# Gate and up projections turned token-major in seven of eleven groups, with a transpose through VectorE and ScalarE

## The chip, the cores and the metric

The kernel runs on one core of one Trainium2 chip. The metric is the device time of one execution in microseconds (us); the lower, the better.

The engines are named as the profile names them: PE is TensorE's matrix multiplication, PEld its weight loads, DVE is VectorE, ACT is ScalarE, POOL is GpSimd and SP is SyncE, which issues the weight transfers here.

## The reference

One layer of a decoder trunk, 256 tokens by 2048 channels, everything in float32. `D_FF` is 5632, which is eleven groups of 512 columns.

```python
def reference(x, p, ...):
    y = _rms(h, norm_mix_g[i])
    z = y @ w_in[i]                      # 2048 x 4096
    ...                                  # four mixers of 512 channels each
    h = h + jnp.concatenate([oa, ob, oc, od], axis=-1) @ w_out[i]
    y = _rms(h, norm_ffn_g[i])
    h = h + (jax.nn.silu(y @ w_gate[i]) * (y @ w_up[i])) @ w_down[i]
    y = _rms(h, norm_ple_g[i])
    h = h + jax.nn.sigmoid(y @ w_ple_gate[i]) * (p[i] @ w_ple_proj[i])
    return _rms(h, final_norm_g)
```

The change lies in the line with `w_gate`, `w_up` and `w_down`.

## The kernel before

**Numbers in two parts.** Each float32 operand is split into a high part, rounded to the format that PE multiplies in (float32r), and a low part, the rest. A product is then three matmuls: high weight by high activation, high weight by low activation, low weight by high activation. For activations `split` (line 102) does this: ACT rounds (`act`, line 66), DVE subtracts (`tt`, line 69). For weights it is done in `load_slab`.

**Slabs and steps.** All weights are streamed once. A step is one slab of weights: four K-tiles of 128 rows by 512 columns, 1 MB. `load_slab` (222) issues the transfer on SP's queue into `raw` (three buffers), has ACT write the high part `whi` (line 266, three buffers) and DVE the low part `wlo` (line 270, three buffers). `run` (398) walks the list `steps`; a slab is loaded when the step two before it begins, and after each step's matmuls `pump` takes deferred work (`defer`, 283) out of the list `bg`, up to the step's budget: it runs a piece while the credit is above minus 2.0 (`OVERDRAFT`) and takes the piece's cost off. `flush` empties the list. That is the order in which the program is written. The framework that compiles it places the waits, and may put an instruction of an engine's queue ahead of one that is written before it.

**Channel-major.** `group` (313) with `wide_out=True` multiplies one group of 512 output channels: for each K-tile `j` and each block `m` of 128 channels, line 335 loads 128 columns of the weight as the stationary operand and streams the activations. With `whi` the moving operand is the high and low part of the activation side by side, 512 columns, into one PSUM bank per `m`; with `wlo` it is the high part alone, 256 columns, into the bank's second half. That is eight matmuls for each K-tile. The result is channels by tokens, four banks a group. Even steps but the last take the 16 products with `whi` first, odd steps and the last those with `wlo`.

**Token-major.** `token_products` (389) has the tokens as the stationary operand (128 tokens of `a`) and streams 512 columns of the weight: `whi`, `wlo`, then `whi` against the low part, for one block `t` of 128 tokens. That is six matmuls of 512 columns for each K-tile and both blocks. The result is tokens by channels. In the kernel before it is used by `group_v`, the first group of the input projection, by `p_last` and by `last_a` and `last_b`, the last group of the gate of the third line.

**The feed-forward part.** `ffn` (759) is called for passes of 3, 3, 3 and 2 groups (`FFN_CUTS`). In a pass each group does four steps of `w_gate`, evacuated by `ev_gate`, and four of `w_up`, evacuated by `ev_up`, which multiplies and splits into `acts`; then four groups of `w_down` with as many steps as the pass has groups use `acts` as the moving operand, channels on the partitions. `hs` holds the split input of the pass, the normalisation's factor by token is in `stats["ffn"]`: element 0 has it with tokens on partitions, element 1 as a row repeated on all partitions. All of `xs`, `mix`, `hs`, `acts`, `hs2` and some smaller things are tiles of the pool `asp`, 28 buffers of 2 KB a partition (line 58).

Of the kernel before, what the change touches and what calls it, by code (L numbers as in the profile page):

```python
# [9 lines left out]
F32 = mybir.dt.float32  # L10
# [22 lines left out]
BUDGET = 2.8  # L33
BUDGET_OUT = 2.8
OVERDRAFT = 2.0
WARM = 9
# [15 lines left out]
def trunk(ctx: ExitStack, tc: tile.TileContext, xT, pT, par, w_in, sgu_wT, sgu_lb, sgu_b,  # L52
# [4 lines left out]
    hp_ = ctx.enter_context(tc.tile_pool(name="resid", bufs=1))  # L57
    asp = ctx.enter_context(tc.tile_pool(name="asp", bufs=28))
    rawp = ctx.enter_context(tc.tile_pool(name="rawp", bufs=3))
# [162 lines left out]
    def load_slab(i, w, k0, nk, cols, hold=False):  # L222
# [21 lines left out]
        if hold:  # L244
            load(0, nk)
            parts = []
            for s in range(nk):
                hi = asp.tile([P, 2, T], F32R, tag="a", name="hold_hi").rearrange("p a t -> p (a t)")
                lo = asp.tile([P, 2, T], F32R, tag="a", name="hold_lo").rearrange("p a t -> p (a t)")
# [14 lines left out]
        for s in range(0, nk, some):  # L264
            e = min(s + some, nk)
            act(hi[:, s:e, :n], raw[:, s:e, :n])
            if i < KD // 4:
                for k in range(4 * i + s, 4 * i + e):
                    xs.append(split(h[k], col("g_mix", k)))
            tt(lo[:, s:e, :n], raw[:, s:e, :n], hi[:, s:e, :n].bitcast(F32), ALU.subtract)  # L270
# [136 lines left out]

    xs = []
    acc1, sums1 = wk("acc", bufs=2), duo(0)
# [109 lines left out]
    def c_out(rows):  # L519
        r = both(rows())  # L520
        for q in range(2):
            tt(cv2[q], cv2[q], r, ALU.mult)
            y, sg = duo(0), duo(0)
            for a in range(2):
                i = 2 * q + a
                act(y[:, a, :], cv2[q][:, a, :], AF.Identity, bias=col("cf_lb", i),
                    scale=col("cf_g", i))
            act(sg, y, AF.Sigmoid)
            tt(y, y, sg, ALU.mult)
            for a in range(2):  # L530
                mix[8 + 2 * q + a] = split(y[:, a, :])

# [59 lines left out]
    def sgu(p, u):  # L592
# [14 lines left out]
        for a in range(2):  # L607
            mix[2 * p + a] = split(o[:, a, :])

# [24 lines left out]
    def evac_bb(p, ps):  # L634
# [5 lines left out]
        for a in range(2):  # L640
            mix[4 + 2 * p + a] = split(o[:, a, :])

# [8 lines left out]
    def pool(p, z):  # L651
# [15 lines left out]
        def project():  # L667
# [4 lines left out]
            for a in range(2):  # L672
                m = 2 * p + a
                mix[12 + m] = split(po[:, a * T:(a + 1) * T], col("pool_s", m))
        defer(0.8, project, 1)
# [47 lines left out]

    hs = [None] * KD
    acc2 = wk("acc", bufs=2)

    def out_group(g, order):
# [6 lines left out]
        def ev_last(p, ps):  # L734
# [3 lines left out]
            for j in (4 * g + 2 * p, 4 * g + 2 * p + 1):  # L738
                hs[j] = split(h[j], col("g_ffn", j))
                square(j, acc2)  # L740
# [14 lines left out]

    hs2 = [None] * KD
    acc3 = wk("acc", bufs=2)

    def ffn(g0, ng, final):
        acts = []  # L760
        gs = {}
# [13 lines left out]
        def ev_up(m, ps):  # L775
# [4 lines left out]
            tt(o, o, gs[m], ALU.mult)  # L780
            acts.append(split(o))

        h4s = lambda i: hs[4 * i:4 * i + 4]
        for g in range(g0, g0 + ng):
            group(w_gate, [(g * GW, GW)], full, h4s, ev_gate, wide_out=True,
                  hooks={i + 1: [f] for i, f in enumerate(stats_hooks(acc2, "ffn"))}
                  if g == 0 else None)
            group(w_up, [(g * GW, GW)], full, h4s, ev_up, wide_out=True)
        for g in range(4):
            def ev(m, ps, g=g):  # L790
                j = 4 * g + m
                add_residual(j, ps)
                if final:
                    hs2[j] = split(h[j], col("g_ple", j))
                    square(j, acc3)
            group(w_down, [(g * GW, GW)], [(4 * g0 + k, 4) for k in range(0, 4 * ng, 4)],
                  lambda i: acts[4 * i:4 * i + 4], ev, wide_out=True,
                  hooks={0: [(lambda: load_p()) if g == 2 else (lambda: p_tiles(0))]}
# [7 lines left out]

    psp = []

    def p_tiles(i):
        if not psp:  # L810
            for k in range(PLE // P):
                psp.append(split(pk[0][:, k, :]))
        return psp
# [35 lines left out]
    def load_g():  # L849
        t = asp.tile([P, 2, T], F32R, tag="a", name="g_row").bitcast(F32)  # L850
        g_row.append(t.rearrange("p a t -> p (a t)"))
        nc.sync.dma_start(out=g_row[0], in_=g_last.broadcast_to([P, GW]))
# [47 lines left out]
    def gate_last(t, q, ps):  # L900

        if q == 0:
            z_last[t] = asp.tile([P, 2, T], F32R, tag="a", name="z_last").bitcast(F32)
            zg_last[t] = wide()
# [107 lines left out]
```

## Time and profile before

| | us |
|---|---|
| median of three runs | 1132.54 (1131.68 to 1132.98) |
| the profiled execution | 1132.19 |
| its span, first to last instruction | 1130.5 |
| PE busy | 1118.4 (99%) |
| DVE busy | 805.5 (71%) |
| ACT busy | 585.0 (52%) |

The span is what the trace covers; 1.7 us of the profiled execution's time lie outside it. A busy share is a share of the span. The granted clock of TensorE is a mean of 0.998 of full speed. Matmuls are pipelined, so the duration of one is longer than the distance from one start to the next; it is the distance that adds up.

### The profile page before, as it was taken

Reading aid. Unit: us, or ns where it says so; the run is one execution under the profiler, and the core shown is the slowest. Engines: PE = TensorE matmul, PEld = TensorE weight load, DVE = VectorE, ACT = ScalarE, POOL = GpSimd, SP = SyncE. Lnnn points to the kernel's source line nnn. Section 1 sums busy time; section 2 is a strip of 40 time slices with the busy share of each in tenths; the row PEclk is TensorE's granted clock in tenths of the full one; section 3 lists DMA queues with packets and bytes.
Section 4 is the critical chain, followed back from the end, with each engine's and each line's share of the span. In section 5 each row is a group of like instructions: output and inputs, shape, how many; then the busy total and the mean of one; then the engine's idle time right before and its main releaser. Section 6 shows DMA issues by size and latency. Waiting matters only on the chain.

```text
span 1130.5 us, 16060 instructions
## 1 busy us (share of the span) xinstructions
PE 1118.4 (99%) x6496; PEld 990.4 (88%) x6496; DVE 805.5 (71%) x1154; ACT 585.0 (52%) x758; POOL 2.2 (0%) x15
## 2 busy tenths in 40 slices
PE   9999999999999999999999999999999999999996
PEld 7888888889888888888888888888888888889886
DVE  7789998969866675567667555766756576786685
ACT  7677677637545453334445333544533354656562
POOL 0000000000000000000000000000000000000000
PEclk9999999999999999999999999999999999999999
DMA  9855555564565646655555565465655555547642
GB/s 311 279 194 188 171 184 169 192 206 159 197 207 170 218 159 199 204 186 185 189 189 184 186 209 193 162 219 170 203 186 187 188 184 194 179 149 233 195 142 75
DMA packets 117290, 214.55 MB, mean 190 GB/s; under 512 B 4320, under 2 KB 19552, under 8 KB 117216
## 3 DMA queue, kind: packets, MB, share of 16 engines
q1 hardware_dynamic: 114640, 212.20, 56.7%
q10 hardware_dynamic: 2576, 1.32, 0.4%
q8 instruction: 51, 0.84, 0.3%
q14 instruction: 23, 0.19, 0.0%
HBM read 211.41 MB, written 2.10 MB: 189 GB/s over the span
## 4 chain that ended last, share of the span: by engine, by line
PE 95%; DVE 2%; ACT 1%; DMA 1%; issue 1%; ACTq 0%; DVEq 0%
PE ps_mm L335 88%; PE ps_mm L338 2%; PE ps_mm L394 1%; PE ps_mm L395 1%; PE ps_mm L393 1%; PE ps_mm L340 1%; DVE wlo L70 1%; ACT whi L67 1%; DMA wide<-sgu_lb 0%; DMA h<-xT 0%; DVE cv L70 0%; ACT duo L67 0%; PE ps_po L670 0%; DVE duo L70 0%; PE ps_sum L190 0%
## 5 line engine op out<-in xcount | busy, mean ns | idle before, releaser
L335 PE MATMUL ps_mm<-a,whi 128*128 128x512 f32 x2944 | 692.0, 391 | 0.2 <-DVE duo L70 0.2
L335 PEld LDWEIGHTS ps_mm<-a,whi 128*128 128x128 f32 x2944 | 544.9, 188 | 109.3 <-DVE duo L70 0.4
L70 DVE TENSOR_TENSOR wlo<-raw,whi 128x2048 fp32r<-128x2048 f32 (+2 forms) x205 | 452.3, 2207 | 249.1 <-ACT whi L67 246.1
L67 ACT ACTIVATE whi<-raw 128x2048 fp32r<-128x2048 f32 (+2 forms) x205 | 378.6, 1847 | 321.6 <-PE ps_mm L335 222.8
L335 PEld LDWEIGHTS ps_mm<-a,wlo 128*128 128x128 f32 x2944 | 368.1, 191 | 8.5
L335 PE MATMUL ps_mm<-a,wlo 128*128 128x256 f32 x2944 | 371.9, 283 | 0.0
L67 ACT ACTIVATE short<-ps_mm 128x256 f32<-128x256 f32 x100 | 37.5, 375 | 79.4 <-PE ps_mm L335 77.9
L70 DVE TENSOR_TENSOR h<-ps_mm,h 128x256 f32<-128x256 f32 (+1 forms) x168 | 61.6, 426 | 3.4 <-PE ps_mm L335 2.9
L70 DVE TENSOR_TENSOR short<-ps_mm,short 128x256 f32<-128x256 f32 x100 | 41.9, 419 | 24.0 <-ACT short L67 22.9
L67 ACT ACTIVATE short<-short 128x256 f32<-128x256 f32 x56 | 23.2, 414 | 64.6 <-DVE short L70 64.5
L70 DVE TENSOR_TENSOR short<-short,r 128x256 f32<-128x256 f32 x100 | 42.3, 423 | 17.7 <-ACT short L67 16.0
L67 ACT ACTIVATE duo<-long_duo,prm 128x256 f32<-128x256 f32 x108 | 45.3, 498 | 1.5 <-DVE duo L70 1.1
L70 DVE TENSOR_TENSOR cv<-cv,duo 128x512 f32<-128x512 f32 x54 | 37.0, 689 | 3.7 <-ACT duo L67 0.7
L70 DVE TENSOR_TENSOR short<-short 128x256 f32<-128x256 f32 x88 | 37.3, 424 | 2.6
L67 ACT ACTIVATE a<-h,prm 128x256 fp32r<-128x256 f32 x32 | 16.0, 501 | 19.6 <-DVE h L70 19.3
L393 PE MATMUL ps_mm<-whi,a 128*128 128x512 f32 (+1 forms) x72 | 25.3, 360 | 0.7 <-ACT a L67 0.7
L394 PE MATMUL ps_mm<-wlo,a 128*128 128x512 f32 (+1 forms) x72 | 25.3, 356 | 0.1
L395 PE MATMUL ps_mm<-whi,a 128*128 128x512 f32 (+1 forms) x72 | 25.3, 356 | 0.0
L338 PE MATMUL ps_mm<-a,whi 128*128 128x256 f32 x88 | 21.5, 283 | 0.0
L340 PE MATMUL ps_mm<-a,whi 128*128 128x256 f32 x88 | 21.5, 284 | 0.0
L67 ACT ACTIVATE a<-short 128x256 fp32r<-128x256 f32 x44 | 17.0, 412 | 3.5 <-DVE short L70 3.5
L67 ACT ACTIVATE short<-h 128x256 f32<-128x256 f32 x41 | 16.5, 403 | 2.7 <-DVE h L70 2.7
(135 smaller groups left out, 397.1 us busy)
## 6 DMA issues: line engine op xcount, KB each, us to landing
raw<-w_gate SPq DMA_DIRECT2D x44, 1024.0 KB, 5.0
raw<-w_up SPq DMA_DIRECT2D x44, 1024.0 KB, 5.0
raw<-w_down SPq DMA_DIRECT2D x44, 1024.0 KB, 5.0
raw<-w_in SPq DMA_DIRECT2D x20, 1024.0 KB, 5.3
raw<-w_out SPq DMA_DIRECT2D x16, 1024.0 KB, 5.1
raw<-w_pg SPq DMA_DIRECT2D x16, 1024.0 KB, 5.1
raw<-w_in SPq DMA_DIRECT2D x36, 256.0 KB, 5.1
raw<-w_in SPq DMA_DIRECT2D x6, 512.0 KB, 6.6
```

The source lines that it names most:

```text
L67: nc.scalar.activation(out, in_, func, bias=bias, scale=scale)
L70: nc.vector.tensor_tensor(out=out, in0=a, in1=b, op=op)
L335: nc.tensor.matmul(o, w, r, start=first, stop=final)
L338: nc.tensor.matmul(o, w, a[:, 0, :], start=first, stop=final and low == 1)
L340: nc.tensor.matmul(o, w, a[:, 1, :], start=False, stop=final)
L393: nc.tensor.matmul(ps, a[:, 0, c], whi[:, x], start=start and j == 0, stop=False)
L394: nc.tensor.matmul(ps, a[:, 0, c], wlo[:, x], start=False, stop=False)
L395: nc.tensor.matmul(ps, a[:, 1, c], whi[:, x], start=False, stop=stop and j == len(tiles) - 1)
```

## The change

Of each pass all groups but the last do gate and up token-major (`group_t`): 2, 2, 2 and 1, together seven of eleven. The last group of each pass stays as it was. `ev_gate_t` and `ev_up_t` evacuate 128 tokens by 512 channels at a time and work on whole banks, with the normalisation's factor as a scalar of the partition. `ev_up_t` rounds and subtracts there, has DVE turn the high and the low part in square blocks of 32 by 32 into `turned`, and defers four pieces for each block of tokens. A piece, `move`, is four ACT copies of 32 partitions by 256 elements, which bring the blocks to the partitions where `w_down` needs them. The steps of the feed-forward groups get a budget of 2.0, and a piece is entered at a cost of 1.0. `hidden` flushes what is left before `w_down` reads. The pool `asp` is cut into 7 buffers of 8 KB instead of 28 of 2 KB, each buffer a quad of four split tiles, and every user of the pool names its place in a quad.

```diff
+BUDGET_FFN = 2.0
-    asp = ctx.enter_context(tc.tile_pool(name="asp", bufs=28))
+    asp = ctx.enter_context(tc.tile_pool(name="asp", bufs=7))
...
+    def quad():
+        return asp.tile([P, 4, 2, T], F32R, tag="a", name="a")
+    class Quads:
+        def __init__(self):
+            self.q = {}
+        def __getitem__(self, k):
+            if k // 4 not in self.q:
+                self.q[k // 4] = quad()
+            return self.q[k // 4][:, k % 4]
-    def split(src, scale=None):
-        a = asp.tile([P, 2, T], F32R, tag="a", name="a")
+    def split(src, a, scale=None):
...
+    def group_t(w, g, evac, hooks=None):
+        ps = []
+        def body(i, parts):
+            if i == 0:
+                ps.extend(bank() for _ in range(TT))
+            for t in range(TT):
+                token_products(ps[t], t, hs[4 * i:4 * i + 4], parts, i == 0, i == 3)
+                if i == 3:
+                    evac(t, ps[t])
+            for f in (hooks or {}).get(i, ()):
+                f()
+        for i in range(KD // 4):
+            steps.append(((w, 4 * i, 4, [(g * GW, GW)]), lambda p, i=i: body(i, p), BUDGET_FFN))
...
+        def ev_gate_t(t, ps):
+            r = stats["ffn"][0][:, t:t + 1]
+            s = wide()
+            act(s, ps, AF.Sigmoid, scale=r)
+            gs[t] = wide()
+            stt(gs[t], ps, r, s, ALU.mult, ALU.mult)
+        def ev_up_t(n):
+            turned = []
+            def f(t, ps):
+                if not turned:
+                    turned.append(asp.tile([P, TT, 2, GW], F32, tag="a", name="turned"))
+                o, hi = gs[t], wide()
+                stt(o, ps, stats["ffn"][0][:, t:t + 1], o, ALU.mult, ALU.mult)
+                act(hi.bitcast(F32R), o)
+                tt(o, o, hi, ALU.subtract)
+                nc.vector.transpose(out=turned[0][:, t, 0, :], in_=hi)
+                nc.vector.transpose(out=turned[0][:, t, 1, :], in_=o)
+                for i in range(4):
+                    defer(1.0, lambda i=i: move(n, t, i, turned[0]))
+            return f
+        def move(n, t, i, turned):
+            acts[4 * n]
+            c = slice(t * P + 32 * i, t * P + 32 * i + 32)
+            for j in range(4):
+                act(acts.q[n][32 * j:32 * j + 32, :, :, c].rearrange("p m s b -> p s m b"),
+                    turned[32 * i:32 * i + 32, t].rearrange(
+                        "p s (m j b) -> p s m j b", m=4, j=4)[:, :, :, j, :])
+        def hidden(i):
+            if bg:
+                flush()
+            return [acts[k] for k in range(4 * i, 4 * i + 4)]
...
-        for g in range(g0, g0 + ng):
-            group(w_gate, [(g * GW, GW)], full, h4s, ev_gate, wide_out=True,
-                  hooks={i + 1: [f] for i, f in enumerate(stats_hooks(acc2, "ffn"))}
-                  if g == 0 else None)
-            group(w_up, [(g * GW, GW)], full, h4s, ev_up, wide_out=True)
+        for n, g in enumerate(range(g0, g0 + ng)):
+            hooks = ({i + 1: [f] for i, f in enumerate(stats_hooks(acc2, "ffn"))}
+                     if g == 0 else None)
+            if n < ng - 1:
+                group_t(w_gate, g, ev_gate_t, hooks)
+                group_t(w_up, g, ev_up_t(n))
+            else:
+                group(w_gate, [(g * GW, GW)], full, h4s, ev_gate, BUDGET_FFN, wide_out=True)
+                group(w_up, [(g * GW, GW)], full, h4s, ev_up, BUDGET_FFN, wide_out=True)
```

## Rows read from the trace of the kernel before

**Rows 1.** Page, busy time: us, share of the span, instructions.

```profile
PE 1118.4 (99%) x6496; PEld 990.4 (88%) x6496; DVE 805.5 (71%) x1154; ACT 585.0 (52%) x758; POOL 2.2 (0%) x15
PEclk9999999999999999999999999999999999999999
```

**Rows 2.** Chain that ended last: by line, then one piece (start, us).

```profile
PE ps_mm L335 88%; PE ps_mm L338 2%; PE ps_mm L394 1%; PE ps_mm L395 1%; PE ps_mm L393 1%; PE ps_mm L340 1%; DVE wlo L70 1%; ACT whi L67 1%; DMA wide<-sgu_lb 0%; DMA h<-xT 0%; DVE cv L70 0%; ACT duo L67 0%; PE ps_po L670 0%; DVE duo L70 0%; PE ps_sum L190 0%
...
302.98 714.31 PE ps_mm L335 x4108
```

**Rows 3.** Timeline of PE, 495 to 550: start, us, instruction, count.

```profile
498.19 4.00 PE L335 MATMUL ps_mm<-a,wlo 128*128 128x256 f32 x32
502.02 7.47 PE L335 MATMUL ps_mm<-a,whi 128*128 128x512 f32 x32
509.33 4.00 PE L335 MATMUL ps_mm<-a,wlo 128*128 128x256 f32 x32
513.16 7.44 PE L335 MATMUL ps_mm<-a,whi 128*128 128x512 f32 x32
520.44 4.00 PE L335 MATMUL ps_mm<-a,wlo 128*128 128x256 f32 x32
...
546.50 3.82 PE L335 MATMUL ps_mm<-a,whi 128*128 128x512 f32 x16
```

**Rows 4.** Timeline of PE, `last_a`: first and after the last of 48 matmuls.

```profile
1096.98 0.39 PE L393 MATMUL ps_mm<-hold_hi,a 128*128 128x512 f32 x1
...
1107.86 0.50 PE L190 MATMUL ps_sum<-ones,acc 128*128 128x1 f32 x4
```

**Rows 5.** Timeline of PE, end of `group_v`: first and after the last of 18 matmuls.

```profile
24.78 0.39 PE L393 MATMUL ps_mm<-whi,a 128*128 128x512 f32 x1
...
28.90 0.62 PE L335 MATMUL ps_mm<-a,whi 128*128 128x512 f32 x2
```

**Rows 6.** Windows of Rows 3, 5 and 4: length, busy us by engine, clock, DMA.

```profile
502.02:546.50 44.48, 44.48 (x258) 39.34 (x257) 29.30 (x37) 20.71 (x24) 0.00 (x0) 1.00 0.56 189
24.78:28.90 4.12, 4.12 (x20) 3.38 (x18) 4.08 (x5) 2.24 (x2) 0.00 (x0) 1.00 0.67 210
1096.98:1107.86 10.88, 10.88 (x49) 9.01 (x48) 7.87 (x17) 6.75 (x14) 0.00 (x0) 1.00 0.00 0
```

**Rows 7.** Groups of ACT by form: count, busy us, mean ns, idle before.

```profile
L67 ACT ACTIVATE whi<-raw 128x2048 fp32r<-128x2048 f32 x191 | 365.6, 1914 | 321.3 <-PE ps_mm L335 222.8 <-DVE h L70 36.5 <-issue 33.1
L67 ACT ACTIVATE a<-short 128x256 fp32r<-128x256 f32 x44 | 17.0, 412 | 3.5 <-DVE short L70 3.5
L67 ACT ACTIVATE wide<-wide 128x512 f32<-128x512 f32 x6 | 3.7, 620 | 0.2 <-DVE wide L70 0.2
L67 ACT ACTIVATE wide<-ps_mm,rsy 128x512 f32<-128x512 f32 x2 | 1.3, 670 | 0.0
```

**Rows 8.** Groups of DVE by form, same columns.

```profile
L70 DVE TENSOR_TENSOR wlo<-raw,whi 128x2048 fp32r<-128x2048 f32 x191 | 437.4, 2290 | 244.3 <-ACT whi L67 241.9 <-DMA raw<-w_in 2.0
L76 DVE SCALAR_TENSOR_TENSOR wide<-wide 128x512 f32<-128x512 f32 x2 | 1.4, 687 | 0.0
L70 DVE TENSOR_TENSOR wide<-wide 128x512 f32<-128x512 f32 x2 | 1.4, 685 | 0.0
```

**Rows 9.** Timeline of ACT, 495 to 550, around the end of a gate group.

```profile
503.15 0.38 ACT L67 ACTIVATE short<-ps_mm 128x256 f32<-128x256 f32 x1 [2.85 <-PE ps_mm L335]
504.48 0.42 ACT L67 ACTIVATE short<-short 128x256 f32<-128x256 f32 x1 [0.95 <-DVE short L70]
504.81 0.36 ACT L67 ACTIVATE short<-ps_mm 128x256 f32<-128x256 f32 x1
505.92 1.91 ACT L67 ACTIVATE whi<-raw 128x2048 fp32r<-128x2048 f32 x1 [0.75 <-ACT short L67]
507.74 0.40 ACT L67 ACTIVATE short<-short 128x256 f32<-128x256 f32 x1
```

**Rows 10.** Timeline of ACT: two copies back to back; a copy and its successor.

```profile
530.37 0.71 ACT L67 ACTIVATE a<-short 128x256 fp32r<-128x256 f32 x2
...
1084.54 0.42 ACT L67 ACTIVATE short<-short 128x256 f32<-128x256 f32 x1 [2.20 <-DVE short L70]
1084.87 0.61 ACT L67 ACTIVATE hold_hi<-raw 128x512 fp32r<-128x512 f32 x1
```

More of the change, by code (lines that the diff above doesn't have):

```diff
@@ L245, in load_slab @@
             load(0, nk)
-            parts = []
+            parts, kept = [], Quads()
             for s in range(nk):
-                hi = asp.tile([P, 2, T], F32R, tag="a", name="hold_hi").rearrange("p a t -> p (a t)")
-                lo = asp.tile([P, 2, T], F32R, tag="a", name="hold_lo").rearrange("p a t -> p (a t)")
+                hi, lo = (kept[2 * s + b].rearrange("p a t -> p (a t)") for b in range(2))
                 act(hi, raw[:, s, :])
@@ L268, in load_slab @@
                 for k in range(4 * i + s, 4 * i + e):
-                    xs.append(split(h[k], col("g_mix", k)))
+                    xs.append(split(h[k], x_parts[k], col("g_mix", k)))
             tt(lo[:, s:e, :n], raw[:, s:e, :n], hi[:, s:e, :n].bitcast(F32), ALU.subtract)
@@ L406, in run @@
             pump(budget)
-    xs = []
+    xs, x_parts, mix_parts = [], Quads(), Quads()
     acc1, sums1 = wk("acc", bufs=2), duo(0)
@@ L530, in c_out @@
             for a in range(2):
-                mix[8 + 2 * q + a] = split(y[:, a, :])
+                mix[8 + 2 * q + a] = split(y[:, a, :], mix_parts[8 + 2 * q + a])
     def gelu2(z, s, g):
@@ L607, in sgu @@
         for a in range(2):
-            mix[2 * p + a] = split(o[:, a, :])
+            mix[2 * p + a] = split(o[:, a, :], mix_parts[2 * p + a])
     hb, cb = {}, {}
@@ L640, in evac_bb @@
         for a in range(2):
-            mix[4 + 2 * p + a] = split(o[:, a, :])
+            mix[4 + 2 * p + a] = split(o[:, a, :], mix_parts[4 + 2 * p + a])
     def evac_d(p, ps):
@@ L673, in project @@
                 m = 2 * p + a
-                mix[12 + m] = split(po[:, a * T:(a + 1) * T], col("pool_s", m))
+                mix[12 + m] = split(po[:, a * T:(a + 1) * T], mix_parts[12 + m], col("pool_s", m))
         defer(0.8, project, 1)
@@ L722, in add_residual @@
         tt(h[j], ps[:, T:], h[j], ALU.add)
-    hs = [None] * KD
+    hs, h_parts = [None] * KD, Quads()
     acc2 = wk("acc", bufs=2)
@@ L738, in ev_last @@
             for j in (4 * g + 2 * p, 4 * g + 2 * p + 1):
-                hs[j] = split(h[j], col("g_ffn", j))
+                hs[j] = split(h[j], h_parts[j], col("g_ffn", j))
                 square(j, acc2)
@@ L753, in trunk @@
             out_group(g, k_order)
-    hs2 = [None] * KD
+    hs2, h2_parts = [None] * KD, Quads()
     acc3 = wk("acc", bufs=2)
+    def group_t(w, g, evac, hooks=None):
[11 more added lines that the diff above has]
+            steps.append(((w, 4 * i, 4, [(g * GW, GW)]), lambda p, i=i: body(i, p), BUDGET_FFN))
     def ffn(g0, ng, final):
-        acts = []
+        acts = Quads()
         gs = {}
@@ L780, in ev_up @@
             tt(o, o, gs[m], ALU.mult)
-            acts.append(split(o))
-        h4s = lambda i: hs[4 * i:4 * i + 4]
-        for g in range(g0, g0 + ng):
-            group(w_gate, [(g * GW, GW)], full, h4s, ev_gate, wide_out=True,
-                  hooks={i + 1: [f] for i, f in enumerate(stats_hooks(acc2, "ffn"))}
-                  if g == 0 else None)
-            group(w_up, [(g * GW, GW)], full, h4s, ev_up, wide_out=True)
+            split(o, acts[4 * (ng - 1) + m])
+        def ev_gate_t(t, ps):
[4 more added lines that the diff above has]
+            stt(gs[t], ps, r, s, ALU.mult, ALU.mult)
@@ L793, in ev @@
                 if final:
-                    hs2[j] = split(h[j], col("g_ple", j))
+                    hs2[j] = split(h[j], h2_parts[j], col("g_ple", j))
                     square(j, acc3)
             group(w_down, [(g * GW, GW)], [(4 * g0 + k, 4) for k in range(0, 4 * ng, 4)],
-                  lambda i: acts[4 * i:4 * i + 4], ev, wide_out=True,
+                  hidden, ev, wide_out=True,
                   hooks={0: [(lambda: load_p()) if g == 2 else (lambda: p_tiles(0))]}
@@ L804, in trunk @@
         g0 += ng
-    psp = []
+    psp, p_parts = [], Quads()
     def p_tiles(i):
@@ L811, in p_tiles @@
             for k in range(PLE // P):
-                psp.append(split(pk[0][:, k, :]))
+                psp.append(split(pk[0][:, k, :], p_parts[k]))
         return psp
@@ L849, in load_g @@
     def load_g():
-        t = asp.tile([P, 2, T], F32R, tag="a", name="g_row").bitcast(F32)
-        g_row.append(t.rearrange("p a t -> p (a t)"))
+        g_row.extend(asp.tile([P, 4, GW], F32, tag="a", name="g_row")[:, i] for i in range(4))
         nc.sync.dma_start(out=g_row[0], in_=g_last.broadcast_to([P, GW]))
@@ L902, in gate_last @@
         if q == 0:
-            z_last[t] = asp.tile([P, 2, T], F32R, tag="a", name="z_last").bitcast(F32)
+            z_last[t] = g_row[1 + t].rearrange("p (a t) -> p a t", a=2)
             zg_last[t] = wide()
```

## The prediction

> **What bounds the kernel now.** I read the busy times first: PE has 1118.4 us of a span of 1130.5, 99%, at full granted clock in every slice; VectorE has 71%, ScalarE 52% [rows 1]. The chain that ended last confirms that PE is not merely busy but the path: 88% of the span are the channel-major matmuls of line 335, and the feed-forward part, the stretch that is changed, is one unbroken piece of 714.31 us and 4108 matmuls [rows 2]. Nothing there ever makes PE wait. So two questions decide: does PE need less time for the same products, and does the new work on the other engines make PE wait where it did not?
>
> **What a channel-major step costs.** The timeline of PE shows blocks of 32 equal matmuls, half a block belonging to one step and half to the next. From the start of the block at 502.02 to the same place one group of gate and up later, 546.50, are 44.48 us, which are eight steps: 5.56 us each [rows 3]. The 512-column block takes 520.44 - 513.16 = 7.28 us, 227.5 ns a matmul; the 256-column block 513.16 - 509.33 = 3.83 us, 119.7 ns [rows 3]. Half the columns cost more than half the time: the 256 columns in between cost 107.8 ns, so about 12 ns of each matmul do not depend on its length.
>
> **What a token-major step costs.** The columns are the same, 3072 for each K-tile, but in six matmuls instead of eight. The kernel already runs this code in two places. In `last_a`, 48 matmuls take 1107.86 - 1096.98 = 10.88 us, 226.7 ns each [rows 4]; at the end of `group_v`, 18 take 28.90 - 24.78 = 4.12 us, 228.9 ns [rows 5]. The windows say how the places differ: no transfers in the first, 210 GB/s and a full VectorE in the second; the feed-forward part has 189 GB/s with VectorE two thirds busy [rows 6]. I take 227.5 ns, between the two and equal to the channel-major matmul of the same length in the very stretch that is changed [rows 3]. A step has 24 of them: 5.46 us, 0.10 less than now. By 56 steps (seven groups, gate and up, four each) the precise difference is 16 x (227.5 + 119.7) - 24 x 227.5 = 95 ns, or **5.3 us**. The ends are 6.4 us (226.7 ns) and 3.5 us (228.9 ns).
>
> Against this step speaks a rule of the Trainium skill, TensorE: Matmul & The Clock Gate, in Part 1 under "Wait — 56ns, not 53.3ns?": back-to-back matmuls cost their columns at 2.4 GHz and a fixed 2.5 ns or so each. By that rule the two matmuls saved for each of 224 K-tiles would be worth an estimated 1.1 us; the rows above show 12 ns where it has 2.5, so here I do not follow it.
>
> **What else leaves the path and what comes onto it.** A group's evacuation gets lighter on VectorE: seven passes of 256 elements for each of four blocks (0.42 us each, some 12 us) become three passes of 512 on two blocks (0.69 each [rows 8], 4.1 us) and four transposes. ScalarE loses 16 short activations and gains two sigmoids from PSUM and two roundings of 512 (0.67 and 0.62 us [rows 7]) and 32 moves. No row shows a transpose or a copy that crosses partitions. For the transpose the nearest row is the 128x512 pass, 0.69 us [rows 8]; ends are 0 and the 2.29 us of a pass four times as long. For the move the nearest row is the ScalarE copy of 256 elements in one direction: 0.41 us of duration [rows 7], but two in a row end after 0.71, and the start of the next instruction follows a copy by 0.33 [rows 10]. I take 0.33 and keep 0.30 to 0.41; a quarter of the partitions gives me no reason for less. The sums: ScalarE 8 x 1.91 + 2.6 + 32 x 0.33 = 28.5 us a group beside 20.7 now [rows 6], out of 43.7; VectorE 8 x 2.29 + 4.1 + 2.8 = 25.2 beside 29.3. Neither becomes the bound. The moves come in a lump, though.
>
> **The lump.** Call the end of an up group's last slab 0 and a step 5.46 us. The slab three steps on may be split from 0, when its `whi` buffer comes free; that takes 1.91 + 2.29 = 4.2 us and a little [rows 7, 8], say 4.3, and PE wants it at 10.9. The slack is 6.6 us. At 0 the first block of tokens, finished 2.7 us earlier, has waited for VectorE's previous subtraction (to about -1.2); product and rounding follow to 0.1, the second block's product and the subtraction to 1.5, two transposes to 2.8 us. Then four pieces of four moves, 16 x 0.33 = 5.3 us, are due, and two more pieces after each of the next two steps. If the split goes first, it is through by 2.0, before the moves can start, and costs nothing. The moves then run from 2.8 to 8.1, two pieces more to 10.7, the next slab's split to 12.6 and its subtraction to 14.9; PE wants that at 16.4, so 1.5 us are left. If the split stands behind the four pieces, it starts at 8.1 and PE waits 1.5 us. The timeline of ScalarE decides for the first: at the end of a gate group a split runs at 505.92, ahead of a sigmoid at 507.74 that is written earlier in the program but was not yet ready [rows 9]. Moves wait for transposes in just that way. I cost the moves at nothing.
>
> The price of a transpose stands in a page as well: the Trainium skill, VectorE: DVE Perf Modes, "The three transpose paths", has 311 ns for 128x128 in bf16. An estimate from that, four times as long for 512 columns, is 1.2 us; it would move the start of the moves from 2.8 to 3.9 us, and no run here shows it yet.
>
> Edits with one answer: the quads hold the same 56 KB. Before the change, 16 small buffers of `hs` and 12 of `acts` fill the pool; after it, four quads of `hs`, and of the three others one for each `acts` quad, with `turned` in a place whose `acts` quad is not needed until the next up group ends. Its eight pieces are all due within three steps, and that is eight steps on. PSUM use falls from four banks a group to two. SP issues the same transfers; a slab's transfer waits for the subtraction that frees `raw`, and that keeps its three-step lead. The flush in `hidden` finds an empty list, since a channel-major group of eight steps stands between the last moves and `w_down`. The budget of the channel-major groups has nothing else to release. The last group of each pass stays channel-major, so `w_down` begins as before. All of these: 0, and if a place were wrong the cost is one wait at one of seven boundaries, of the size below.
>
> **Sum.** 1132.2 us of the profiled execution, less 5.3, plus nothing: 1126.9. The median lies 0.35 above that execution, so 1127.2 by the median.
>
> **Rivals.** First, *PE waits at the boundaries for a split that stands behind the moves*. Three boundaries lead into another token-major group, which wants `wlo` with its second matmul; four into a channel-major one, which takes 16 products with `whi` first, so only the split itself, 1.91 us, must be there. With m for one move, PE waits 2.8 + 16m - 6.6 at the three and 2.8 + 16m - 9.0 at the four, where positive. At m = 0.33 that is 3 x 1.5 = 4.5 us, and the gain left is 0.8: **1131.7**, no change that can be told. For it: the first four pieces are written ahead of the slab. Against it: rows 9.
>
> Second, *slower: the same queue with moves at their full duration*. At 0.41 us, 16m is 6.6: 3 x 2.8 + 4 x 0.4 = 10 us of waits against 5.3 gained: **1137.2**. It decides from m = 0.35 us, where 3 x (16m - 3.8) reaches 5.3. With moves of 0.41 and the split first, the second slab's split would end at 14.6 and its subtraction at 16.9, 0.5 late at each of seven boundaries, 3.5 us: again no change. For it: 32 moves a group is ScalarE's largest new item, and no row shows one. Against it: rows 10 and rows 9.
>
> Third, *it doesn't shorten PE's work*: the fixed part of a matmul is hidden where operand and weights change roles. A token-major matmul then takes 5.56 us / 24 = 231.5 ns and the gain is nothing: **1132.5**. Rows 4 and 5 speak against it, with 226.7 and 228.9. The Trainium skill's TensorE: Matmul & The Clock Gate, in the section named above, comes near this rival with its estimated 1.1 us.
>
> **How the numbers follow.** A measurement of this kernel tells some 0.2%, 2.3 us, from no change. Forecast, 0.60, with its own range from 1126.1 to 1129.0 (3.5 to 6.4 us gained): all faster. First rival 0.15 and third 0.04, both the same. Second 0.21: 0.19 slower, and 0.02 the same for its milder form. So faster 0.60, same 0.21, slower 0.19. The range for 8 in 10 begins a little under the forecast's best end, 1125.3, and ends with the second rival, 1137.5; out of it are moves dearer than 0.41 us.
>
> **What would show it.** Right: in a token-major step 24 matmuls at 227 to 228 ns from start to start, a step of 5.46 us; the feed-forward part still one piece of PE in the chain; moves 0.30 to 0.35 us apart; a split at the end of an up group ahead of the first move. Wrong: a PE row of lines 393 or 394 with idle time before it released by `wlo` or `whi`, two or three steps after an up group, and a split released by a move; or matmuls of lines 393 to 395 spaced by more than 231 ns, which would eat the whole gain, since 24 of them would then take what 32 take now.

## The result and the profile after

| | us |
|---|---|
| before, beside the changed kernel | 1132.76 (1131.68 to 1133.52, 4 runs) |
| changed | 1145.97 (1145.39 to 1146.78, 4 runs) |
| changed : before | 1.0118 (1.01 to 1.0135) |
| profiled execution of the changed kernel, its span | 1146.52, 1144.8 |

The change makes the kernel 13.2 us slower. It was forecast 5.3 us faster, and the range ended at 1137.5. The page answers to [rows 1] and [rows 2] with these lines, busy time first and then the chain that ended last, by engine and by line:

```profile
PE 1116.4 (98%) x6048; PEld 967.5 (85%) x6048; DVE 772.2 (67%) x1028; ACT 654.7 (57%) x898; POOL 2.7 (0%) x15
PE 85%; ACT 6%; DVE 5%; issue 3%; DMA 1%; ACTq 0%; DVEq 0%
PE ps_mm L348 56%; PE ps_mm L407 9%; PE ps_mm L408 9%; PE ps_mm L406 8%; ACT a L68 3%; ACT whi L68 2%; DVE wlo L71 2%; PE ps_mm L351 2%; PE ps_mm L353 1%; DMA wide<-sgu_lb 1%; DMA h<-xT 0%; DVE cv L71 0%; DVE short L71 0%; DVE h L71 0%; ACT duo L68 0%
```

PE is busy for 2.0 us less than before, but the chain is no longer PE's alone: the moves (`ACT a`, 3%) have entered it, and the splits of weights (`ACT whi`, `DVE wlo`) and the issue of instructions have grown in it. Where the 14.3 us of the span went is read from a landmark that both kernels have, the sums over tokens of a norm on PE (start, us). The first two lines are of the kernel before, the next three of the changed one; the third landmark of before is the last line of [rows 4]:

```profile
293.39 0.50 PE L190 MATMUL ps_sum<-ones,acc 128*128 128x1 f32 x4
1025.76 0.50 PE L190 MATMUL ps_sum<-ones,acc 128*128 128x1 f32 x4
```

```profile
293.84 0.50 PE L204 MATMUL ps_sum<-ones,acc 128*128 128x1 f32 x4
1037.48 0.50 PE L204 MATMUL ps_sum<-ones,acc 128*128 128x1 f32 x4
1119.60 0.50 PE L204 MATMUL ps_sum<-ones,acc 128*128 128x1 f32 x4
```

Up to the first landmark the kernels differ by 0.45 us. The feed-forward part between the first two takes 743.64 in place of 732.37 us, **+11.27**. The next stretch is the same within 0.02. From the last landmark to the end of the span it is 25.20 in place of 22.64, **+2.56**. Two places, then.

**The feed-forward part.** The products themselves are quicker, as the timeline of PE shows ahead of the first boundary between two token-major groups (first and last start of 114 equal distances, and what follows):

```profile
317.73 0.39 PE L406 MATMUL ps_mm<-whi,a 128*128 128x512 f32 x1
...
343.57 0.39 PE L406 MATMUL ps_mm<-whi,a 128*128 128x512 f32 x1
344.63 0.50 PE L407 MATMUL ps_mm<-wlo,a 128*128 128x512 f32 x1 [0.67 <-DVE wlo L71]
344.97 0.40 PE L408 MATMUL ps_mm<-whi,a 128*128 128x512 f32 x1
```

25.84 us / 114 are 226.7 ns, which makes a step 0.114 us shorter than a channel-major one. Two of the 56 token-major steps lie ahead of the first landmark; over the other 54 this is 54 x 0.114 = 6.2 us less. So waits must have cost 11.27 + 6.2 = 17.5 us. The list of PE's waits (us, times, longest) has 13.8 of them, in 15 places, and there was none of these three kinds in the feed-forward part before:

```profile
PE ps_mm L348 <- DVE short L71: 9.6, 8, 1.6
...
PE ps_mm L348 <- DVE wlo L71: 2.2, 4, 0.6
PE ps_mm L407 <- DVE wlo L71: 2.0, 3, 0.7
```

A wait costs more than the idle time beside it: the one above, 0.67 us long, puts 0.83 us between the starts at 343.57 and 344.63 that were not there, and 0.11 more up to the next, 0.27 beyond what is listed. The starts around the other 14 waits say 0.26 or 0.27 as well. For 15 waits that is 4.0, and 13.8 + 4.0 = 17.8, within 0.4 us of what is needed.

What the waits wait for stands in ScalarE's timeline at the next boundary, from a token-major up group, whose last matmul starts at 371.53, to a channel-major gate group. It answers to the place of [rows 9]:

```profile
371.46 0.63 ACT L68 ACTIVATE wide<-wide 128x512 fp32r<-128x512 f32 x1 [3.02 <-DVE wide L77]
372.01 1.92 ACT L68 ACTIVATE whi<-raw 128x2048 fp32r<-128x2048 f32 x1
373.83 0.61 ACT L68 ACTIVATE wide<-wide 128x512 fp32r<-128x512 f32 x1
374.56 10.25 ACT L68 ACTIVATE a<-turned 32x256 fp32r<-32x256 f32 x24
384.84 1.92 ACT L68 ACTIVATE whi<-raw 128x2048 fp32r<-128x2048 f32 x1
386.78 3.39 ACT L68 ACTIVATE a<-turned 32x256 fp32r<-32x256 f32 x8
390.19 3.72 ACT L68 ACTIVATE whi<-raw 128x2048 fp32r<-128x2048 f32 x2
393.82 0.37 ACT L68 ACTIVATE short<-ps_mm 128x256 f32<-128x256 f32 x1
```

One split goes first, at 372.01, as forecast. Then come 24 moves, six pieces, in one row: 10.25 us, 0.427 a move, where 0.33 was taken and 0.41 was the upper end. The next split ends at 386.76, and the same place of VectorE and PE reads:

```profile
386.79 2.29 DVE L71 TENSOR_TENSOR wlo<-raw,whi 128x2048 fp32r<-128x2048 f32 x1 [8.23 <-ACT whi L68]
392.14 4.49 DVE L71 TENSOR_TENSOR wlo<-raw,whi 128x2048 fp32r<-128x2048 f32 x2 [3.06 <-ACT whi L68]
396.55 0.42 DVE L71 TENSOR_TENSOR short<-ps_mm,short 128x256 f32<-128x256 f32 x1
```

```profile
389.13 2.17 PE L348 MATMUL ps_mm<-a,wlo 128*128 128x256 f32 x16 [0.56 <-DVE wlo L71]
391.14 4.27 PE L348 MATMUL ps_mm<-a,whi 128*128 128x512 f32 x18
397.02 2.57 PE L348 MATMUL ps_mm<-a,whi 128*128 128x512 f32 x10 [1.61 <-DVE short L71]
399.43 2.19 PE L348 MATMUL ps_mm<-a,wlo 128*128 128x256 f32 x17
402.40 1.19 PE L348 MATMUL ps_mm<-a,whi 128*128 128x512 f32 x4 [0.78 <-DVE short L71]
```

PE gets the low part at 389.1 in place of 388.4. That is the smaller part of the loss. The larger part comes after it: eight more moves, two late splits and two late subtractions stand ahead of the evacuation of the gate group, whose first addition runs at 396.55. There are six banks for products. The gate group holds four of them, and the up group wants four: it starts in the two that are free and then waits twice, for 1.61 and 0.78 us.

**The tail.** The first sigmoid of the last gate group had its products at 1119.6, but ran 7 us later (the first line shows the engine's instruction before it):

```profile
1117.58 0.51 ACT L68 ACTIVATE h<-h,prm 128x256 f32<-128x256 f32 x1
1126.73 1.20 ACT L68 ACTIVATE g_row<-ps_mm,rsy 128x256 f32<-128x256 f32 x3 [8.63 <-PE ps_mm L408]
```

In the kernel before it ran beside the products of `last_b`. The code gives the reason that the runs below tested: `g_row.extend(asp.tile(...)[:, i] for i in range(4))` calls the pool once for each `i`. Four quads are taken where one was meant; with four quads of `hs2` and two of held weights the seven places don't suffice, and `z_last` waits for one to come free in the middle of `last_b` (the sixth product of its second half, the last to read the first held quad, starts at 1126.41).

### The profile page after: what moved, and what is told of

Same layout as the page of the kernel before. It is cut to its first block, busy times and chain, and to the rows that moved or that the text cites. A ratio compares the mean times of both kernels' runs of the same rounds, so it can differ in the third digit from the quotient of the medians.

```text
span 1144.8 us, 15164 instructions
## 1 busy us (share of the span) xinstructions
PE 1116.4 (98%) x6048; PEld 967.5 (85%) x6048; DVE 772.2 (67%) x1028; ACT 654.7 (57%) x898; POOL 2.7 (0%) x15
## 4 chain that ended last, share of the span: by engine, by line
PE 85%; ACT 6%; DVE 5%; issue 3%; DMA 1%; ACTq 0%; DVEq 0%
PE ps_mm L348 56%; PE ps_mm L407 9%; PE ps_mm L408 9%; PE ps_mm L406 8%; ACT a L68 3%; ACT whi L68 2%; DVE wlo L71 2%; PE ps_mm L351 2%; PE ps_mm L353 1%; DMA wide<-sgu_lb 1%; DMA h<-xT 0%; DVE cv L71 0%; DVE short L71 0%; DVE h L71 0%; ACT duo L68 0%
## 5 line engine op out<-in xcount | busy, mean ns | idle before, releaser
L348 PE MATMUL ps_mm<-a,whi 128*128 128x512 f32 x2048 | 485.7, 391 | 9.8 <-DVE short L71 9.6
L348 PEld LDWEIGHTS ps_mm<-a,whi 128*128 128x128 f32 x2048 | 378.3, 188 | 87.3 <-DVE short L71 12.1
L348 PEld LDWEIGHTS ps_mm<-a,wlo 128*128 128x128 f32 x2048 | 257.6, 191 | 9.7 <-DVE wlo L71 3.0
L348 PE MATMUL ps_mm<-a,wlo 128*128 128x256 f32 x2048 | 261.5, 283 | 2.2 <-DVE wlo L71 2.2
L407 PE MATMUL ps_mm<-wlo,a 128*128 128x512 f32 (+1 forms) x520 | 200.0, 385 | 2.1 <-DVE wlo L71 2.0
L406 PE MATMUL ps_mm<-whi,a 128*128 128x512 f32 (+1 forms) x520 | 199.8, 386 | 0.7 <-ACT a L68 0.7
L408 PE MATMUL ps_mm<-whi,a 128*128 128x512 f32 (+1 forms) x520 | 199.6, 384 | 0.0
L407 PEld LDWEIGHTS ps_mm<-wlo,a 128*128 128x128 f32 x520 | 97.6, 188 | 23.1 <-DVE wlo L71 4.2
L406 PEld LDWEIGHTS ps_mm<-whi,a 128*128 128x128 f32 x520 | 97.7, 188 | 20.7 <-ACT a L68 1.6
L408 PEld LDWEIGHTS ps_mm<-whi,a 128*128 128x128 f32 x520 | 97.7, 188 | 19.6 <-DVE a L77 0.2
L68 ACT ACTIVATE a<-turned 32x256 fp32r<-32x256 f32 x224 | 93.1, 415 | 3.4
L68 ACT ACTIVATE short<-ps_mm 128x256 f32<-128x256 f32 x44 | 16.4, 372 | 22.4 <-PE ps_mm L348 22.0
L71 DVE TENSOR_TENSOR short<-short,r 128x256 f32<-128x256 f32 x44 | 18.6, 423 | 6.7 <-ACT short L68 6.0
```

The lines of the kernel that those rows point to most:

```text
L68: nc.scalar.activation(out, in_, func, bias=bias, scale=scale)
L71: nc.vector.tensor_tensor(out=out, in0=a, in1=b, op=op)
L348: nc.tensor.matmul(o, w, r, start=first, stop=final)
L406: nc.tensor.matmul(ps, a[:, 0, c], whi[:, x], start=start and j == 0, stop=False)
L407: nc.tensor.matmul(ps, a[:, 0, c], wlo[:, x], start=False, stop=False)
L408: nc.tensor.matmul(ps, a[:, 1, c], whi[:, x], start=False, stop=stop and j == len(tiles) - 1)
```

## Experiments

Two theories stood at the start. A: the 32 moves on ScalarE, in lumps ahead of the splits and of the channel-major evacuation, make PE wait. B: it is something else that came with them, the transposes and passes on VectorE or the coarser pool. The differences below are medians against the kernel before in the same sitting (1132.05 to 1132.54); the changed kernel stands at +13.2.

**One quad for the row of gains.**

```diff
-        g_row.extend(asp.tile([P, 4, GW], F32, tag="a", name="g_row")[:, i] for i in range(4))
+        q = asp.tile([P, 4, GW], F32, tag="a", name="g_row")
+        g_row.extend(q[:, i] for i in range(4))
```

> The changed kernel with one edit: the row of the last norm's gains and the two blocks of z_last lie in one quad. In the changed kernel a generator calls the pool four times, so that four quads are taken; with four of hs2 and two of held weights that is more than the seven there are, and the first sigmoid of the last gate group waits until the last product has read the first held quad (1126.73 in its trace, where the result was there at 1119.6). Theory: the whole loss of the tail, 2.6 us of the span, comes back: 1143.4 against 1146.0, and that sigmoid starts within 0.3 us of the end of its products. Rival, that the tail is later because of the order of the last steps or a changed queue: no change, 1146.

1143.18 us, +11.0. The sigmoids now run as soon as their products are there, at 1118.89, 0.2 us after this kernel's last landmark at 1118.69 (in the changed kernel it was 7 us):

```profile
1118.89 0.84 ACT L68 ACTIVATE g_row<-ps_mm,rsy 128x256 f32<-128x256 f32 x2 [1.70 <-PE ps_mm L408]
```

The span falls by 3.2 us, from 1144.8 to 1141.6: 2.3 in the tail (22.91 in place of 25.20), the rest ahead of the first landmark. The feed-forward part is unchanged (743.66 us). The four quads are the cause of the tail's loss.

**The pool's cut alone.**

All eleven groups are channel-major again; the pool in quads, the row of gains and the steps' budget stay as in the changed kernel.

```diff
-            split(o, acts[4 * (ng - 1) + m])
+            split(o, acts[4 * n + m])
...
-            if n < ng - 1:
+            if False:
...
```

> The pool in quads alone: all eleven groups channel-major, as in the kernel before, with the users of the pool, the four quads of the gains' row and the steps' budget of the changed kernel. Theory: the feed-forward part is as before, and only the tail is late: 1132.8 + 2.6 = 1135.4. Rival, that coarser buffers make PE wait in the feed-forward part too (a share of the 17.9 us): 1138 or more; that the tail's loss comes from the token-major groups: 1132.8.

1135.11 us, +3.0, ratio 1.0027 (1.0015 to 1.004). The feed-forward part, between the landmarks at 292.70 and 1024.95, takes 732.25 us, as before. So the quads cost nothing there; the tail's sigmoid has the same 8.63 us of waiting ahead of it. Theory B loses the pool.

**The same work on VectorE, a quarter of the moves.** The copies take all 128 partitions and leave the blocks where they are.

```diff
-            for j in range(4):
-                act(acts.q[n][32 * j:32 * j + 32, :, :, c].rearrange("p m s b -> p s m b"),
-                    turned[32 * i:32 * i + 32, t].rearrange(
-                        "p s (m j b) -> p s m j b", m=4, j=4)[:, :, :, j, :])
+            act(acts.q[n][:, :, :, c].rearrange("p m s b -> p s m b"),
+                turned[:, t].rearrange("p s (m j b) -> p s m j b", m=4, j=4)[:, :, :, i, :])
```

> The changed kernel with 8 copies of 128 partitions by 256 elements a group in place of 32 of 32 partitions; the blocks are not moved between partitions, so that part of the computation is left out. Everything on VectorE, the budget and the pool is as in the changed kernel. Theory, that ScalarE's 32 moves cause the waits in the feed-forward part: they go, 1146.0 - 17.9 = 1128. Rival, that the transposes, the longer passes on VectorE or the pool of quads cause them: 1143 to 1146. The distance between two such copies in a row (0.43 us for the moves of the changed kernel, 0.33 for copies of 128 partitions in the kernel before) tells whether the access pattern (eight runs of 32 elements) has a price: 0.33 if not, 0.43 if so.

1127.76 us, -4.4 with the tail's loss still in it; ratio 0.9961 (0.9946 to 0.9976). None of the three kinds of wait is left in PE's list. The transposes are the same, 0.70 and 0.67 us. So A holds and B falls. The copies also give the clue to the price of a move:

```profile
330.37 1.34 ACT L68 ACTIVATE a<-turned 128x256 fp32r<-128x256 f32 x4
```

Four in 1.34 us, the last 0.40 long, are 0.31 from start to start. The access pattern is that of the moves; it has no price.

**Moves that stay on their partitions, and moves that stay on one quarter.** A quarter is 32 of the 128 partitions. Both kernels have 32 copies of 32 partitions and do not bring the blocks to their places. In the first, the copies of a piece go from quarter `j` to quarter `j`, so that two in a row change the quarter; in the second all four go from quarter `i` to quarter `i`.

```diff
-                    turned[32 * i:32 * i + 32, t].rearrange(
+                    turned[32 * j:32 * j + 32, t].rearrange(
```

> The changed kernel with 32 moves a group of 32 partitions each that stay on their partitions (quarter j to quarter j); the blocks are not brought to their places, so that part of the computation is left out. If a move's 0.43 us from start to start come from the crossing of partitions, the distance falls to the 0.31 us of copies of 128 partitions and the time to some 1135; if they come from a copy's using 32 partitions, or from two in a row that use different ones, it stays 0.43 and the time 1146.

```diff
-            c = slice(t * P + 32 * i, t * P + 32 * i + 32)
...
-                act(acts.q[n][32 * j:32 * j + 32, :, :, c].rearrange("p m s b -> p s m b"),
+                c = slice(t * P + 32 * j, t * P + 32 * j + 32)
+                act(acts.q[n][32 * i:32 * i + 32, :, :, c].rearrange("p m s b -> p s m b"),
```

> The changed kernel with the moves of a piece all on one quarter of the partitions, from it and to it; the blocks are not brought to their places, so that part of the computation is left out. The moves that change nothing but their partitions stood 0.43 us apart. If that is because two in a row use different quarters, the distance within a piece falls to 0.31 us; if it is because a copy uses 32 partitions instead of 128, it stays 0.43 and the time 1145.

The first is at 1144.70 (+12.2), 24 moves in 10.25 us as in the changed kernel. The second is at 1131.02 (-1.0). There is one run of each, but the distances can be read from its trace. The second's lump at the same boundary:

```profile
372.72 8.07 ACT L68 ACTIVATE a<-turned 32x256 fp32r<-32x256 f32 x24
380.81 1.92 ACT L68 ACTIVATE whi<-raw 128x2048 fp32r<-128x2048 f32 x1
```

The five distances at which the quarter changes are 0.41 us in this trace and the last copy is 0.40 long, so that the other 18 distances are (8.07 - 0.40 - 2.05) / 18 = 0.31 us. It is neither the crossing nor the 32 partitions: two ScalarE copies in a row overlap while they use the same partitions, and not at all when the quarter changes. And 2.2 us less in the lump of 24, with 0.7 less in the eight behind it, are worth some 14 us of the kernel's time: the waits for `wlo` are all gone, of the waits for a bank one of 0.60 us is left at each of four places.

**The same moves with one target a piece.** A piece has one target quarter and four sources, in place of one source and four targets.

> The changed kernel with the same 32 moves in another order: a piece has one quarter of the partitions as its target and takes its four copies from the four quarters, where the changed kernel has one source and four targets. Copies that stay on one quarter overlapped (0.31 us apart), copies that changed both source and target quarter did not (0.43), and nor did those with one source and four targets. If the target alone decides, the moves of a piece stand 0.31 us apart, 24 of them take 8.1 us in place of 10.3, and the time is that of the kernel whose pieces stayed on one quarter, 1131. If any change of quarter decides, they stay 0.43 apart and the time is 1146.

1145.59, +13.4, ratio 1.0118 (1.0101 to 1.0135), 24 moves in 10.25 us. A change of the source alone is enough to lose the overlap, as a change of the target alone was in the changed kernel. For moves between quarters no order keeps both, except where consecutive copies repeat the same pair, which no run tried.

**The moves spread.** A piece is entered at twice the cost, so that the budget lets fewer of them out after a step.

```diff
-                    defer(1.0, lambda i=i: move(n, t, i, turned[0]))
+                    defer(2.0, lambda i=i: move(n, t, i, turned[0]))
```

> The changed kernel with one number changed: a piece of four moves is entered at a cost of 2.0 instead of 1.0, so that 12 moves instead of 24 stand on ScalarE's queue ahead of the split of the slab four steps on. The work is the same. Theory, that PE's new waits (17.9 us in the feed-forward part, each with the restart of PE behind it) come from the lump of moves ahead of that split: the split starts some 5 us earlier, the waits for wlo and for PSUM banks go, and the time is 1146.0 - 17.9 = 1128. Rival, that the sum of the moves or the transposes on VectorE is what is too much, wherever they stand: the waits stay, 1143 to 1146.

1140.56, +8.4, ratio 1.0077 (1.0059 to 1.0094): a third of what was expected. The waits for `wlo` went, as the theory has it, with 12 moves ahead of the split. The waits for banks stayed, 8.6 us in 8 places. ScalarE's timeline shows why:

```profile
377.94 1.92 ACT L68 ACTIVATE whi<-raw 128x2048 fp32r<-128x2048 f32 x1
379.89 4.27 ACT L68 ACTIVATE a<-turned 32x256 fp32r<-32x256 f32 x10
384.18 1.91 ACT L68 ACTIVATE whi<-raw 128x2048 fp32r<-128x2048 f32 x1
386.12 2.55 ACT L68 ACTIVATE a<-turned 32x256 fp32r<-32x256 f32 x6
388.69 1.92 ACT L68 ACTIVATE whi<-raw 128x2048 fp32r<-128x2048 f32 x1
390.63 1.70 ACT L68 ACTIVATE a<-turned 32x256 fp32r<-32x256 f32 x4
392.35 0.39 ACT L68 ACTIVATE short<-ps_mm 128x256 f32<-128x256 f32 x1
```

The engine is never free from the boundary on, and the last four moves stand right ahead of the gate group's evacuation. A lump made smaller but longer reaches the next thing that has a date, that is, an instruction whose result PE will want at a time that is set.

At one of the four boundaries PE lost clock as well. The same 13 matmuls behind the same two waits (0.5 and 1.7 us) read as follows at the second boundary into a channel-major group and at the third:

```profile
596.40 3.26 PE L348 MATMUL ps_mm<-a,whi 128*128 128x512 f32 x13 [1.67 <-DVE short L71]
797.34 4.80 PE L348 MATMUL ps_mm<-a,whi 128*128 128x512 f32 x13 [1.66 <-DVE short L71]
```

From 797.32 to 800.73 the granted clock is 0.50 (1.2 GHz), and 1.0 at the other three places. So 1.5 us of the profiled execution's time are clock; the fall came right behind the waits, at one place of four.

**Fewer, longer moves.** Both blocks of tokens go in one copy of 512 elements, 16 a group, and a piece is entered at a cost of 4.0 once both are turned; with one quad for the gains.

```diff
...
+            for j in range(4):
+                act(acts.q[n].rearrange("p m s (t c) -> p m (s t) c", t=TT)[
+                        32 * j:32 * j + 32, :, :, 32 * i:32 * i + 32],
+                    turned.rearrange("p s t (m j b) -> p m (s t) j b", m=4, j=4)[
+                        32 * i:32 * i + 32, :, :, j, :])
...
```

> One quad for the gains' row, as before, and 16 moves of 32 partitions by 512 elements a group in place of 32 by 256: both blocks of tokens go in one copy, after both are turned. Theory, that each move pays its full duration because copies of 32 partitions do not overlap, and that their sum ahead of a split and ahead of the channel-major evacuation is what PE waits for: a move takes about 0.63 us (0.62 is the 128x512 copy), the sum falls from 13.7 to 10.1 us a group, at most 11 stand ahead of a split (7 us instead of 10.3), all are done before the next channel-major gate group is evacuated. PE's waits in the feed-forward part go: 1132.2 - 7 = 1125, faster than the kernel before. Rival, that in the spread kernel the PSUM waits came from the channel-major evacuation's own length: they stay, some 2.6 us at four places, and the time is 1135.

1130.65, -1.9, ratio 0.9985 (0.9976 to 0.9993), between what was expected (1125) and the rival (1135). A move takes 0.63 us, and at the boundary into a channel-major group 11 stand ahead of a split. They start two microseconds later, since both blocks must have been turned, and the evacuation behind them is still late once in each of four groups:

```profile
376.66 7.03 ACT L68 ACTIVATE a<-turned 32x512 fp32r<-32x512 f32 x11
```

```profile
395.03 3.24 PE L348 MATMUL ps_mm<-a,whi 128*128 128x512 f32 x13 [0.99 <-DVE short L71]
```

**Half of the moves, and all of them, on VectorE.** Both kernels have one quad for the gains and the entry cost of 2.0. The lines are those of the first; in the second, every move goes by VectorE.

```diff
...
+                if j % 2:
+                    nc.vector.tensor_copy(out=o, in_=x)
+                else:
+                    act(o, x)
...
```

> One quad for the gains' row, the higher entry cost of a piece, and every second of the 32 moves on VectorE. Theory of the lump on ScalarE: 16 moves of 0.43 us are 6.9 us a group there; VectorE gets 16 copies of 32 partitions by 256, for which no trace has a row (0.2 to 0.45 us each, 3 to 7 us of some 14 idle in a group). PE's waits go and the time is 1125 as with long moves. Rival, that VectorE is as tight as ScalarE at the boundary, since it must write the low part of the same slab: waits for wlo in place of those for the split, 1130 to 1138.

> One quad for the gains' row, the higher entry cost, and all 32 moves on VectorE, where one is 0.29 us and they stand 0.30 apart. Theory that a lump counts by its length ahead of a slab's split or subtraction, whichever engine it is on: 32 x 0.30 = 9.5 us, with VectorE at 34 of 43.6 us a group, behind the transposes and ahead of the subtraction of the next slabs; the slack of a subtraction is 6.6 us, so that some waits for wlo come back where more than 20 moves stand ahead of one: 1127 to 1133, later than with half the moves on each engine (1125.0). Rival, that only ScalarE's queue matters: 1125 or less.

Half: **1125.0 us (1124.6 to 1125.3), -7.5, ratio 0.9934 (0.9921 to 0.9948)**, quicker than both kernels. PE has none of the three waits. Three edits are in this kernel, and no run has the sharing alone; the kernel with the moves spread would be at some 1138 without the tail's 2.6 us (an estimate), so most of the gain over it is the sharing's. VectorE's row at the first boundary:

```profile
337.42 2.99 DVE L846 CAST a<-turned 32x256 fp32r<-32x256 f32 x10
340.44 2.29 DVE L71 TENSOR_TENSOR wlo<-raw,whi 128x2048 fp32r<-128x2048 f32 x1
```

Ten copies in 2.99 us, 0.30 each. All on VectorE: 1141.16, +9.1, ratio 1.0081 (1.0064 to 1.0098), outside what I expected. The waits for `wlo` did not come back, those for banks did, more than in the kernel with the moves spread:

```profile
PE ps_mm L348 <- DVE short L71: 11.0, 8, 1.7
```

At the same boundary as above, ScalarE's part of the evacuation ran as soon as the products were there, and VectorE's addition only behind the last moves:

```profile
390.76 0.39 ACT L68 ACTIVATE short<-ps_mm 128x256 f32<-128x256 f32 x1 [2.80 <-PE ps_mm L348]
```

```profile
393.87 0.59 DVE L845 CAST a<-turned 32x256 fp32r<-32x256 f32 x2
394.49 0.43 DVE L71 TENSOR_TENSOR short<-ps_mm,short 128x256 f32<-128x256 f32 x1
```

The clock of this trace, too, fell to 0.50 once, for 3.4 us from 958.82, behind waits of 1.08 and 1.66 us. A lump hurts on either engine; the evacuation of a channel-major group passes through both.

## Why the prediction was wrong

**The cost of a token-major step** was right in its mechanism and a little small. 226.7 ns in place of 227.5 make the gain 6.4 us where 5.3 were forecast; the value of `last_a` [rows 4] was the better choice, though the stretch has transfers. In the kernel with half of the moves on VectorE, where PE waits for none of this, the feed-forward part takes 1018.34 - 292.62 = 725.7 us, 6.6 less than before. The rule of the Trainium skill that was weighed there (TensorE: Matmul & The Clock Gate, Part 1), with an estimated 1.1 us, does not agree with that.

**The step that failed is the lump**, where the prediction said "I cost the moves at nothing". It failed in two of its terms.

First, the price of a move: 0.427 us, where 0.33 was taken, and above the upper end of 0.41. The bound was the duration of a copy, and the value the distance of two copies of 128 partitions [rows 10]. That ScalarE's copies overlap only on the same partitions stood in no row, and bounds taken from one kind of copy did not cover it. The Trainium skill says in ScalarE: Activation LUTs, "What ACT_TABLE_LOAD costs", that consecutive activations overlap by about 93 ns; the traces agree for copies on the same partitions (0.40 long, 0.31 apart), and disagree for those that change quarter (0.415 long, 0.427 apart).

The rest of that working held. Counted from the end of the up group's last slab (371.76, one distance behind its last start) the first split goes ahead, the moves begin at 2.8 and 24 of them stand ahead of the second split, all as forecast. They end at 13.05 in place of 10.7, which is the price alone (24 x 0.1), and so the second subtraction ends at 17.3 in place of 14.9, where PE wants it at 16.65 (16.4 in the forecast). These are the seven waits for `wlo`, 4.2 us in the list.

Second, and larger: who else queues behind the lump. "Edits with one answer" names PSUM use and finds that it falls. At the four boundaries into a channel-major group it doesn't: there the gate group uses four banks and the up group wants four of six at once, and the additions that free them stand on the two engines that the lump has made late. Of the 13.8 us of listed waits, 9.6 are of this kind. The prediction priced a wait for `whi` and `wlo` at those places, and none for a bank.

How the two go together shows in the kernel whose moves stay on one quarter. Its 24 copies stand (8.07 - 0.40) / 23 = 0.33 us apart on average, the price taken, and it has one wait of 0.60 us at each of the four places, with the restart some 3.5 us in all (an estimate). That much the omission would have cost at the price taken, and the price did the rest. Without the tail's 2.6 us that kernel would be at some 1128.4 (an estimate), inside the forecast's own range of 1126.1 to 1129.0. No run puts the evacuation ahead of the late splits and leaves the moves as they are, so what the order alone is worth was not measured.

**The tail** is a reading error. "The quads hold the same 56 KB" counts the pool's bytes and not how many quads the row of gains takes; the code takes four, which cost 2.6 us of the span.

**The rivals.** The second had the direction and the engine, with a threshold of 0.35 us for a move; a move was dearer than its worst case. Its place was off: the first split did not stand behind the moves. Its milder form had that right, with the second subtraction 0.5 us late at each of seven boundaries; the trace has 0.56 to 0.67 us at the seven. It called that no change, since it had no wait for a bank. The first rival put its wait at the first split, where there was none; that its 4.5 us lie near the 4.2 listed for `wlo` is luck. The third fell: the products did get shorter.

## What to carry to other kernels

Where PE is the chain, an edit that shortens its work also shortens the date of everything behind it; before counting the gain, write down for each engine that gets new work what queues behind it with a date, evacuations that free banks included. A lump matters by its length ahead of the next dated instruction: 10.3 us in one row brought 13.8 us of listed waits and 8.1 us brought 2.4, and the same moves shared by two engines brought none and made the kernel quicker than before. And a new kind of instruction has no bound from its nearest relative until a row shows how two of them in a row stand.

## What the runs showed of the hardware

- Two ScalarE copies of 256 elements in a row stand 0.31 us apart where they use the same partitions, whether 128 or one quarter; where source or target quarter changes they stand 0.41 to 0.43 apart, a little more than the duration of the first. Crossing partitions adds nothing to that: 24 copies take 10.25 us with it and without.
- VectorE's transpose of 128x512 in blocks of 32 by 32 takes 0.67 to 0.71 us, as much as an addition of that size (0.69). The estimate of 1.2 us from the Trainium skill (VectorE: DVE Perf Modes, "The three transpose paths") was too high.
- A VectorE copy of 32 partitions by 256 elements takes 0.29 us and stands 0.30 from the next where the target quarter changes; no run has two in a row on the same quarters. Here VectorE moves such a block more cheaply than ScalarE.
- A wait of PE in a stream costs about 0.27 us beyond the idle time listed: 0.16 ahead of the first matmul behind it and 0.1 in that matmul's own distance to the next.
- Behind two waits of PE close together (0.48 and 1.66 us; 1.08 and 1.66 us) the granted clock fell from 1.0 to 0.50 for 3.4 us once in each of two traces, and 13 matmuls took 4.80 and 4.85 us in place of 3.26 and 3.24; at the three other places of each trace with the same waits it stayed at 1.0.
